# Three changes of order in a hybrid encoder layer: where weight sums are made, when v's tiles are asked for, and where the sums of the branches stand

## The chip, the cores and the metric

The kernel runs on one core of one Trainium2 chip. The metric is the device time of one execution in microseconds. An execution uses five engines: TensorE (PE, matmuls and transposes), VectorE (DVE), ScalarE (ACT), GpSimd (POOL), and SyncE (SP), which here only issues DMAs. Each engine takes its instructions in its own order, and waits at an instruction until what it needs is there.

## The reference

One layer of an encoder, for one sequence of 1024 tokens of width 2048, all in fp32:

```python
h = rmsnorm(x, pre_g) * (1.0 + scale[:, None]) + shift[:, None]   # scale, shift, gate from c
proj = h @ w_in                                                   # 2048 x 4608
q, k, v, gate_a, u, gate_p = jnp.split(proj, SPLIT_POINTS, axis=-1)
y_a = windowed_gqa(q, k, v, rel_table, sink) * jax.nn.silu(gate_a)
y_p = multiscale_pool(u, w_pool_grp, pool_scale) * jax.nn.silu(gate_p)
g = jax.nn.sigmoid(h @ w_merge + b_merge)                         # 2048 x 4096
g_a, g_p = jnp.split(g, N_BRANCHES, axis=-1)
merged = g_a * (y_a @ w_br_attn) + g_p * (y_p @ w_br_pool)        # each 1024 x 2048
o = merged @ w_out                                                # 2048 x 2048
return x + gate[:, None] * rmsnorm(o, post_g)
```

`windowed_gqa` has 8 query heads and 2 key/value heads of 128 and sees 128 tokens to each side; `multiscale_pool` averages over windows of 2, 4, 8 and 16 tokens.

## The kernel before

**Products.** A fp32 operand is split into a high part (`whi`, `T1h`, made by ACT, L95) and a low part (`wlo`, `T1l`, made by DVE, L96), and a product takes three matmuls for each K-tile: high by high, low by high, high by low. Blocks of 2 x 2 are multiplied with seven products instead of eight (`strassen`, L210): B11, T3, T2, B21, T4, T1 and B22, named after the moving operand. Each has four K-tiles of 128 x 512, so 12 matmuls. One call handles one pair of 128-wide columns. Before the products, the weights are combined (`ws`, sums over `raw`, L102 and L105); after them, the results in the banks X, V and Z are read and added into tiles `u`, `p` and `c`, and stored. The matmuls are on L235. The `u<-V,u` of these pages is the sum that reads T4's result from bank V and so frees the bank for the T3 product of the next pair.

**Stages.** Pass 1 (`pass1`, L607) multiplies the first half of the K-tiles of `w_in` and `w_merge` and stores partial sums in `part_d`. In its last pairs, the *x stage*, the second half of x is brought in: `fetch_x` loads a tile `xt` (L762) and scales it on ACT (L763), `turn_x` transposes it on PE (L769) and copies the result out (L772). Tiles `xt` have three buffers, and a tile is loaded two steps ahead of its turn. Pass 2 multiplies the second half of the K-tiles, adds the partial sums and stores `proj_d`; attention and pooling run beside it as further small steps. The attention's k and v are taken by `take_kv`, which loads 128 x 512 tiles `kvr` (L823) and, for v, transposes them (L828). At the end of pass 2 the rows of the attention branch (`ya_d`) are loaded as tiles `y` (L1026) and their operand sums are made (`pre_op`, L147 and L1030). Then come the two branch products, `w_branch_attn` (beside which the pooled branch's tiles, from `yp_d`, are loaded and summed) and `w_branch_pool`, each with gates `gt` (load L1096, sigmoid L1102) that `finish` multiplies with the results (L1112, L1116). The last product, by `w_out`, uses sums of its weights that were made earlier.

**Sums of weights.** `weight_sums` (L629) makes those: `fetch` loads four tiles `sw` of `w_out` (L638), `make` forms four sums on DVE in a pinned order, `put_by` stores them to `ws_d` (L650). `lay_out` says at which product each of the three runs:

```python
for at, step in zip((0, 5, 7), sums.popleft()):
    steps.setdefault(first + (last - first) * k // n + at, []).append(step)
```

With seven products to a pair, `first` 0 and `last` 35 mean that the k-th group of sums is fetched at the first product of pair k, made at its sixth and stored at the first of the next pair.

**Who sets the order.** `run` (L321) calls one product after the other, and behind each the steps that were laid out for it and, for the indices in `every`, one step of a queue `side`. In the x stage `every` is `(0, 1, 2, 4, 5, 6)`: the fourth product has no step of x. The tile framework then schedules each engine's instructions from the traced program. `keep` (L90) pins an instruction: it may not be moved ahead of the instruction of its engine that was traced before it. SP issues all the loads and stores in one queue.

Of the kernel before, what the change touches and what calls it, by code (L numbers as in the profile page):

```python
# [12 lines left out]
F32 = mybir.dt.float32  # L13
F32R = mybir.dt.float32r
AF = mybir.ActivationFunctionType
ALU = mybir.AluOpType
# [4 lines left out]
P = 128  # L21
# [21 lines left out]
def encoder_layer(ctx: ExitStack, tc: tile.TileContext, x, c, table, w_ada, b_ada, pre_g,  # L43
# [32 lines left out]
    def uid(s):  # L76
        cnt[0] += 1
        return f"{s}_{cnt[0]}"
# [11 lines left out]
    def keep(ins):  # L90

        tc.keep_in_program_order(ins)
# [11 lines left out]
    def sub(o, a, b):  # L104
        return nc.vector.tensor_tensor(o, a, b, ALU.subtract)  # L105
# [38 lines left out]
    def new_op(n=4):  # L144
        return {m: [None] * n for m in MOVING}

    def pre_op(j, h1, h2, tmp):  # L147

        sub(h1[j][1], h1[j][1], h1[j][0])
        t2 = tmp()  # L150
        sub(t2, h2[j][1], h1[j][1])
        return t2

    def fill_op(op, js, h1, h2, t2, now=3):
# [452 lines left out]
    def pass1(n, side, every, steps={}):  # L607

        nonlocal i
        for k in range(n):  # L610
            if not ready:
                fetch_pair(i)
            at = [(at, step) for at in range(7) for step in steps.get(7 * k + at, ())]
            if i + 1 < PAIRS:
                at.append((2, lambda i=i: fetch_pair(i + 1)))
            w, n0 = weight_of(ORDER[i])
            run(strassen(w, n0, rows_in_turn(0), range(4), op, ev, to_dram(block(part_d, ORDER[i])),
                         raws=ready.pop(0)), side, every[k % len(every)], at)
            i += 1
        flush()  # L620
# [115 lines left out]
    def lay_out(n, first, last):  # L736

        steps = {}
        for k in range(n):
            for at, step in zip((0, 5, 7), sums.popleft()):  # L740
                steps.setdefault(first + (last - first) * k // n + at, []).append(step)
        assert max(steps) < last + 2
        return steps
# [43 lines left out]
        t2[j] = pre_op(j, h1, h2, lambda: wsp.tile([P, 512], F32, tag="sw", name=uid("tf")))  # L787

    side.extend(lambda j=j: pre(j) for j in range(4))
    pass1(PAIRS - i, side, ((0, 1, 2, 4, 5, 6),), lay_out(5, 0, 35))  # L790
    assert not side and not sums


# [17 lines left out]
    mid.close()  # L811

    with pool("attn") as ap:
        kv = {}

        def take_kv(kvh, what):
            hi = ap.tile([P, S], F32R, tag=what + "hi", name=uid(what))
            lo = ap.tile([P, S], F32R, tag=what + "lo", name=uid(what))
            col = (COL_K if what == "k" else COL_V) + kvh * P
            for s in range(2):  # L820
                sl = slice(s * 512, (s + 1) * 512)
                raw = ap.tile([P, 512], F32, tag="raw", name=uid("kvr"), bufs=2)
                load(raw, proj_d[col:col + P, sl])  # L823
                src = raw
                if what == "v":
                    src = bank("at")
                    for j in range(4):
                        nc.tensor.transpose(src[:, j * P:(j + 1) * P], raw[:, j * P:(j + 1) * P], ident)  # L828
                split(hi[:, sl], lo[:, sl], src)
            kv[what] = (hi, lo)  # L830
# [85 lines left out]
        def step(u, e):  # L916
            nu = len(UNITS)
            if e == 0 and 0 <= u - LAG_V < nu:
                values(u - LAG_V)
            if 0 <= u - LAG_T < nu:  # L920
                turn(u - LAG_T, e)
            if u < nu:
                if u % 16 == 0 and e == 0:
                    take_kv(UNITS[u][0] * 2 // GQA, "k")
                if u % 4 == 0:
                    split_q(e)
                scores(u, e)
            if e == 1:
                if u % 4 == 3 and u + 1 < nu:
                    fetch_q(u + 1)  # L930
                c_ = u - LAG_V + 1
                if 0 <= c_ < nu:
                    if c_ % 16 == 0:
                        take_kv(UNITS[c_][0] * 2 // GQA, "v")
                    if c_ % 4 == 0:
                        open_gate(c_)
# [86 lines left out]
    def y_steps(yd, store_to):  # L1023
        def get(k, s):
            t = sp.tile([P, 512], F32, tag="y", name=uid("y"), bufs=16)
            load(t, yd[k * P:(k + 1) * P, s * 512:(s + 1) * 512])  # L1026
            h1, h2, _ = store_to
            (h1 if k < 4 else h2).setdefault(k % 4, []).append(t)

        def pre(j):  # L1030
            h1, h2, t2 = store_to
            t2[j] = pre_op(j, h1, h2, lambda: sp.tile([P, 512], F32, tag="tf", name=uid("tf"), bufs=4))

        return [lambda k=k, s=s: get(k, s) for k in (0, 4, 1, 5, 2, 6, 3, 7) for s in range(2)] + \
            [lambda j=j: pre(j) for j in range(4)]
# [28 lines left out]
    for b, w in enumerate((w_ba, w_bp)):  # L1064
        op = new_op()
        fill_op(op, range(4), *ys[b], now=7 if b else 3)
        if b == 0:
            side.extend(y_steps(yp_d, ys[1]))
        else:
            ysrc.close()  # L1070
            ev_ctx.close()
            ev_ctx = ExitStack()
            ev = ctx.enter_context(pool("ev4", 4, side="right"))
            mr = ctx.enter_context(pool("mraw", side="right"))

# [12 lines left out]
            mt, mt2 = merged_tiles(), {}  # L1088
            side.extend([lambda: None] * 25)
            for jp in range(JP - 1):  # L1090
                side[6 * jp + 7] = lambda jp=jp: merged_sums(mt, mt2, jp)
        gates, shut = {}, deque()

        def fetch_gate(i, blk, b=b):
            gt = ev.tile([P, 512], F32, tag="gt", name=uid("gt"), bufs=4)
            load(gt, block(proj_d, NIN + b * D + i * 256)(blk))  # L1096
            gates[i, blk] = gt
            shut.append((gt, 64 + b * KT + 2 * i + (1 if blk[0] == "2" else 0)))

        def open_gate():  # L1100
            gt, col = shut.popleft()
            nc.scalar.activation(gt, gt, AF.Sigmoid, bias=cols[:, col:col + 1])  # L1102

        wanted = deque((i, blk) for i in range(8) for blk in ("11", "21", "22", "12"))
        for _ in range(4):
            fetch_gate(*wanted.popleft())

        for i in range(8):
            def finish(blk, ps, addend, res, gates=gates, shut=shut, open_gate=open_gate, i=i, b=b):
                gt = gates.pop((i, blk))  # L1110
                if ps is not None and addend is None:
                    nc.vector.tensor_tensor(res, ps, gt, ALU.mult)  # L1112
                else:
                    if ps is not None:
                        add(res, ps, addend)
                    nc.vector.tensor_tensor(res, res, gt, ALU.mult)  # L1116
                if b == 0:
                    store(block(mp_d, i * 256)(blk), res)
                else:
                    if blk[1] == "1":  # L1120
                        dst = mt[int(blk[0]) - 1][i // 2][:, i % 2]
                    else:
                        dst = ev.tile([P, 512], F32, tag="pv", name=uid("pv"), bufs=2)
                    load(dst, block(mp_d, i * 256)(blk))
                    add(dst, dst, res)
                    if blk[1] == "2":
                        store(block(m_d, i * 256)(blk), dst)
                if shut:
                    open_gate()
                if wanted:  # L1130
                    fetch_gate(*wanted.popleft())

            at = [(n, open_gate) for n in (0, 1, 2, 3)] if i == 0 else []
            if b == 1 and i == 7:
                at += [(1 + jp, lambda jp=jp: put_op(0, jp, ops[0], mt, mt2)) for jp in range(JP - 1)]
                at += [(5, lambda: merged_sums(mt, mt2, JP - 1)), (5, lambda: put_op(0, JP - 1, ops[0], mt, mt2))]
            run(strassen(w, i * 256, rows_apart, range(4), op, ev, finish), side,
                () if b == 0 and i == 0 else (0, 2, 4) if b == 0 or i < 7 else (0, 1, 2, 3), at)
        flush()
        assert not side  # L1140
# [292 lines left out]
```

## Time and profile before

| what | value |
|---|---|
| median of 3 runs | 2140.0 us (2134.43 to 2148.4) |
| the profiled execution | 2138.01 us, span 2136.2 us |
| granted TensorE clock, mean | 0.998 |
| busy, share of the span | PE 98%, DVE 72%, ACT 53% |
| DMA | 466.10 MB, mean 218 GB/s |

Times in the profile count from the start of the span. A row of a timeline reads: start, duration, engine, line, operation, output and inputs, count, and in brackets the idle time of the engine before it with what ended that time. A wait is charged to the last thing that arrived.

### The profile page before, as it was taken

Reading aid. Unit: us, or ns where it says so; the run is one execution under the profiler, and the core shown is the slowest. Engines: PE = TensorE matmul, PEld = TensorE weight load, DVE = VectorE, ACT = ScalarE, POOL = GpSimd, SP = SyncE. Lnnn points to the kernel's source line nnn. Section 1 sums busy time; section 2 is a strip of 40 time slices with the busy share of each in tenths; the row PEclk is TensorE's granted clock in tenths of the full one; section 3 lists DMA queues with packets and bytes.
Section 4 is the critical chain, followed back from the end, with each engine's and each line's share of the span. In section 5 each row is a group of like instructions: output and inputs, shape, how many; then the busy total and the mean of one; then the engine's idle time right before and its main releaser. Section 6 shows DMA issues by size and latency. Waiting matters only on the chain.

```text
span 2136.2 us, 28939 instructions
## 1 busy us (share of the span) xinstructions
PE 2094.8 (98%) x9567; PEld 1715.6 (80%) x9567; DVE 1537.5 (72%) x2754; ACT 1129.4 (53%) x2124; POOL 7.4 (0%) x66
## 2 busy tenths in 40 slices
PE   6999999999999999999999999999999999999998
PEld 3588888888878888888888888878788888788886
DVE  5786666777547677777776888656966977879667
ACT  5654444444474546767775433333645644767655
POOL 0000000000000000000000000000000000000000
PEclk9999999999999999999999999999999999999999
DMA  9886567899676355545445766765654655696997
GB/s 328 269 274 216 187 202 230 300 310 305 214 228 205 119 174 198 169 152 193 157 157 166 231 219 208 229 189 172 222 172 163 220 191 164 212 306 219 301 304 252
DMA packets 303254, 466.10 MB, mean 218 GB/s; under 512 B 23882, under 2 KB 144866, under 8 KB 303104
## 3 DMA queue, kind: packets, MB, share of 16 engines
q1 hardware_dynamic: 301648, 462.02, 66.4%
q0 software_dynamic: 1120, 2.19, 0.3%
q8 instruction: 75, 1.23, 0.2%
q14 instruction: 75, 0.61, 0.1%
q10 hardware_dynamic: 336, 0.06, 0.0%
HBM read 340.41 MB, written 125.85 MB: 218 GB/s over the span
## 4 chain that ended last, share of the span: by engine, by line
PE 89%; DMA 5%; DVE 4%; ACT 1%; issue 1%; SPq 0%; DVEq 0%; ACTq 0%
PE Z L235 30%; PE V L235 20%; PE X L235 20%; PE Z L1163 2%; PE Z L1164 2%; PE Z L1165 2%; PE V L1165 1%; PE V L1163 1%; PE V L1164 1%; PE X L1165 1%; PE X L1164 1%; PE GEMV L453 1%; PE X L1163 1%; DVE wlo L96 1%; DMA xt<-in_x_dram 1%
## 5 line engine op out<-in xcount | busy, mean ns | idle before, releaser
L95 ACT ACTIVATE whi<-raw 128x512 fp32r<-128x512 f32 (+1 forms) x528 | 319.8, 609 | 502.0 <-PE Z L235 254.3
L96 DVE TENSOR_TENSOR wlo<-raw,whi 128x512 fp32r<-128x512 f32 (+1 forms) x528 | 347.6, 663 | 192.6 <-PE Z L235 118.0
L96 DVE TENSOR_TENSOR wlo<-wr,whi 128x512 fp32r<-128x512 f32 x224 | 151.2, 689 | 59.0 <-ACT whi L95 54.9
L95 ACT ACTIVATE whi<-wr 128x512 fp32r<-128x512 f32 x224 | 138.6, 629 | 90.1 <-DVE wlo L96 31.4
L102 DVE TENSOR_TENSOR raw<-raw,raw 128x512 f32<-128x512 f32 x80 | 55.2, 690 | 95.1 <-DMA raw<-in_w_merge_dram 69.3
L1102 ACT ACTIVATE gt<-gt,cols 128x512 f32<-128x512 f32 x64 | 46.1, 722 | 95.3 <-DMA gt<-proj_d 83.3
L235 PE MATMUL V<-T3h,whi 128*128 128x512 f32 x336 | 92.3, 393 | 1.8 <-DVE u L102 1.8
L235 PE MATMUL X<-B11h,whi 128*128 128x512 f32 x336 | 92.5, 393 | 1.1 <-DVE part L102 1.0
L235 PE MATMUL Z<-B22h,whi 128*128 128x512 f32 x336 | 92.4, 395 | 0.6 <-ACT u L290 0.6
L235 PE MATMUL Z<-T1h,whi 128*128 128x512 f32 x336 | 91.5, 391 | 0.6 <-ACT T1h L95 0.6
L235 PE MATMUL Z<-T2h,whi 128*128 128x512 f32 x336 | 92.0, 393 | 0.0
L235 PE MATMUL V<-T4h,whi 128*128 128x512 f32 x336 | 91.5, 391 | 0.4 <-ACT T4h L95 0.4
L102 DVE TENSOR_TENSOR u<-V,u 128x512 f32<-128x512 f32 x94 | 64.7, 688 | 37.7 <-PE V L235 37.0
L235 PE MATMUL V<-T3h,wlo 128*128 128x512 f32 x336 | 91.4, 392 | 0.0
L235 PE MATMUL Z<-T2l,whi 128*128 128x512 f32 x336 | 91.4, 392 | 0.0
L235 PE MATMUL Z<-T1l,whi 128*128 128x512 f32 x336 | 90.9, 390 | 0.3 <-DVE T1l L96 0.3
L235 PE MATMUL V<-T3l,whi 128*128 128x512 f32 x336 | 91.0, 391 | 0.0
L235 PE MATMUL X<-B21h,whi 128*128 128x512 f32 x336 | 91.0, 391 | 0.0
L235 PE MATMUL Z<-T2h,wlo 128*128 128x512 f32 x336 | 90.9, 391 | 0.0
L235 PE MATMUL V<-T4l,whi 128*128 128x512 f32 x336 | 90.9, 390 | 0.0
L235 PE MATMUL X<-B11l,whi 128*128 128x512 f32 x336 | 90.9, 390 | 0.0
L235 PE MATMUL Z<-B22l,whi 128*128 128x512 f32 x336 | 90.7, 390 | 0.0
(306 smaller groups left out, 4872.4 us busy)
## 6 DMA issues: line engine op xcount, KB each, us to landing
part<-part_d SPq DMA_DIRECT2D x136, 256.0 KB, 5.0
ada<-in_w_ada_dram SPq DMA_DIRECT2D x128, 256.0 KB, 5.4
raw<-in_w_in_dram SPq DMA_DIRECT2D x64, 512.0 KB, 4.1
raw<-in_w_merge_dram SPq DMA_DIRECT2D x64, 512.0 KB, 5.6
wr<-ws_dS SPq DMA_DIRECT2D x64, 512.0 KB, 5.2
wr<-in_w_out_dram SPq DMA_DIRECT2D x48, 512.0 KB, 5.1
proj_d<-part SPq DMA_DIRECT2D x68, 256.0 KB, 2.2
sw<-in_w_out_dram SPq DMA_DIRECT2D x64, 256.0 KB, 5.3
```

The lines of the kernel that those rows point to most:

```text
L95: ins = (nc.scalar.activation(hi, src, AF.Copy), nc.vector.tensor_tensor(lo, src, f32(hi), ALU.subtract))
L96: nc.vector.tensor_tensor(lo, src, f32(hi), ALU.subtract))
L102: return (eng or nc.vector).tensor_tensor(o, a, b, ALU.add)
L235: nc.tensor.matmul(ps, w_[:, i], op[mov][j][m_], start=fresh and i == 0 and n == 0, stop=i == nj - 1 and n == 2, skip_group_check=True)
L453: ins = nc.tensor.matmul(pv[g:g + 32, :], scz[:, kc, :], tile_of(kc), start=kc < 4, stop=kc >= 12, tile_position=(0, g))
L1102: nc.scalar.activation(gt, gt, AF.Sigmoid, bias=cols[:, col:col + 1])
L1163: nc.tensor.matmul(pb, hi, w[0], start=first, stop=False, skip_group_check=True)
L1164: nc.tensor.matmul(pb, lo, w[0], start=False, stop=False, skip_group_check=True)
L1165: nc.tensor.matmul(pb, hi, w[1], start=False, stop=last, skip_group_check=True)
```

## The change

There are three edits. First, the weight sums of the x stage move by three products: `lay_out(5, 0, 35)` becomes `lay_out(5, 3, 38)`, so that a group is fetched at the fourth product of a pair, made at the second product of the next and stored at its fourth. Second, the raw tiles of v are loaded by a new `fetch_v`, called one step before `take_kv` uses them. Third, the sums of `y` and the multiplies by the gates are pinned with `keep`: `pre_op` gets a parameter `pin`, which the x stage leaves empty.

```diff
-    def pre_op(j, h1, h2, tmp):
-
-        sub(h1[j][1], h1[j][1], h1[j][0])
+    def pre_op(j, h1, h2, tmp, pin=lambda ins: None):
+
+        pin(sub(h1[j][1], h1[j][1], h1[j][0]))
         t2 = tmp()
-        sub(t2, h2[j][1], h1[j][1])
+        pin(sub(t2, h2[j][1], h1[j][1]))
         return t2
...
-    pass1(PAIRS - i, side, ((0, 1, 2, 4, 5, 6),), lay_out(5, 0, 35))
+    pass1(PAIRS - i, side, ((0, 1, 2, 4, 5, 6),), lay_out(5, 3, 38))
...
-        kv = {}
+        kv, vraw = {}, []
+
+        def fetch_v(kvh):
+            for s in range(2):
+                vraw.append(ap.tile([P, 512], F32, tag="raw", name=uid("kvr"), bufs=2))
+                load(vraw[s], proj_d[COL_V + kvh * P:COL_V + (kvh + 1) * P, s * 512:(s + 1) * 512])
...
-                raw = ap.tile([P, 512], F32, tag="raw", name=uid("kvr"), bufs=2)
-                load(raw, proj_d[col:col + P, sl])
-                src = raw
-                if what == "v":
-                    src = bank("at")
+                if what == "k":
+                    src = raw = ap.tile([P, 512], F32, tag="raw", name=uid("kvr"), bufs=2)
+                    load(raw, proj_d[COL_K + kvh * P:COL_K + (kvh + 1) * P, sl])
+                else:
+                    raw, src = vraw.pop(0), bank("at")
...
                 c_ = u - LAG_V + 1
+                if (c_ + 1) % 16 == 0 and c_ + 1 < nu:
+                    fetch_v(UNITS[c_ + 1][0] * 2 // GQA)
...
-            t2[j] = pre_op(j, h1, h2, lambda: sp.tile([P, 512], F32, tag="tf", name=uid("tf"), bufs=4))
+            t2[j] = pre_op(j, h1, h2, lambda: sp.tile([P, 512], F32, tag="tf", name=uid("tf"), bufs=4), keep)
...
-                    nc.vector.tensor_tensor(res, ps, gt, ALU.mult)
+                    keep(nc.vector.tensor_tensor(res, ps, gt, ALU.mult))
...
-                    nc.vector.tensor_tensor(res, res, gt, ALU.mult)
+                    keep(nc.vector.tensor_tensor(res, res, gt, ALU.mult))
```

No instruction is added or removed on PE, DVE, ACT or SP; their order changes in three places. In the attention stage no row changes its place.

**Place one: SP in the x stage**, around the loads of the sixth and seventh x tile. Before, where these are called `xt_5500` and `xt_5544` (`sw` are weights and their sums, `raw` weights of the pass, `ws_dS_95` to `ws_dS_98` the four sums in memory):

```order
L762 DMA xt_5500<-in_x_dram 128x512
L311 DMA part_d<-u_1128_5411 128x512
L650 DMA ws_dS_97<-sw_5345 128x512
L650 DMA ws_dS_96<-sw_5463 128x512
L650 DMA ws_dS_95<-sw_5343 128x512
L650 DMA ws_dS_98<-sw_5349 128x512
L311 DMA part_d<-p_1120_5372 128x512
L638 DMA sw_5536<-in_w_out_dram 128x512
L638 DMA sw_5538<-in_w_out_dram 128x512
L638 DMA sw_5540<-in_w_out_dram 128x512
L638 DMA sw_5542<-in_w_out_dram 128x512
L762 DMA xt_5544<-in_x_dram 128x512
```

With the change, where the same two tiles are called `xt_5495` and `xt_5527`:

```order
L650 DMA ws_dS_97<-sw_5407 128x512
L650 DMA ws_dS_96<-sw_5559 128x512
L650 DMA ws_dS_95<-sw_5405 128x512
L311 DMA part_d<-u_1124_5403 128x512
L762 DMA xt_5495<-in_x_dram 128x512
L187 DMA raw_5597<-in_w_merge_dram 128x4x256
L762 DMA xt_5527<-in_x_dram 128x512
L311 DMA part_d<-p_1116_5364 128x512
L650 DMA ws_dS_98<-sw_5411 128x512
L638 DMA sw_5635<-in_w_out_dram 128x512
L762 DMA xt_5564<-in_x_dram 128x512
L638 DMA sw_5637<-in_w_out_dram 128x512
```

The second tile's load stood behind four stores of sums and four loads of weights, and now stands ahead of the store of `p`, the fourth store and all the loads; the first tile's load now stands behind three stores and the store of `u`. On DVE three or four of a group's four sums, which all stood behind `u<-V,u`, now stand ahead of it: they are pinned behind the low part of the weights of the next pair's T3 product (`wlo<-ws`), which is prepared that early.

**Place two: DVE at the end of pass 2**, around `u<-V,u` of the pair in which the attention branch's sums are traced. Before:

```order
L105 TENSOR_TENSOR y_13066<-y_13066,y_13044 128x512
L102 TENSOR_TENSOR u_2593_12948<-V_12856,u_2593_12948 128x512
L96 TENSOR_TENSOR wlo_13069<-raw_12844,whi_13068 128x512
L105 TENSOR_TENSOR tf_13411<-y_13109,y_13066 128x512
L96 TENSOR_TENSOR wlo_13091<-raw_13012,whi_13090 128x512
L102 TENSOR_TENSOR p_2586_12892<-p_2586_12892,u_2600_13004 128x512
L105 TENSOR_TENSOR y_13150<-y_13150,y_13130 128x512
L96 TENSOR_TENSOR wlo_13112<-raw_13014,whi_13111 128x512
```

With the change:

```order
L105 TENSOR_TENSOR ws_13208<-raw_13174 128x512
L102 TENSOR_TENSOR u_2593_12948<-V_12856,u_2593_12948 128x512
L96 TENSOR_TENSOR wlo_13069<-raw_12844,whi_13068 128x512
L96 TENSOR_TENSOR wlo_13091<-raw_13012,whi_13090 128x512
L102 TENSOR_TENSOR p_2586_12892<-p_2586_12892,u_2600_13004 128x512
L96 TENSOR_TENSOR wlo_13112<-raw_13014,whi_13111 128x512
```

All eight sums (four `y<-y,y`, four `tf<-y,y`) have left this pair and the next; they stand some 30 to 50 rows further down, in the pair after.

**Place three: the pooled branch's sums.** On DVE in the first pair of `w_branch_attn`, before:

```order
L105 TENSOR_TENSOR tf_15253<-y_14564,y_14447 128x512
L96 TENSOR_TENSOR T4l_14249<-y_13271,T4h_14248 128x512
L1112 TENSOR_TENSOR c_14311<-X_14179,gt_14167 128x512
L96 TENSOR_TENSOR T4l_14253<-y_13368,T4h_14252 128x512
L105 TENSOR_TENSOR y_14653<-y_14653,y_14608 128x512
L96 TENSOR_TENSOR T1l_14279<-y_13066,T1h_14278 128x512
L102 TENSOR_TENSOR u_2869_14276<-V_14181,u_2869_14276 128x512
```

With the change:

```order
L96 TENSOR_TENSOR T4l_14249<-y_13271,T4h_14248 128x512
L1118 TENSOR_TENSOR c_14311<-X_14179,gt_14167 128x512
L96 TENSOR_TENSOR T4l_14253<-y_13368,T4h_14252 128x512
L96 TENSOR_TENSOR T1l_14279<-y_13066,T1h_14278 128x512
L96 TENSOR_TENSOR wlo_14387<-raw_14379,whi_14386 128x512
L96 TENSOR_TENSOR T1l_14283<-y_13150,T1h_14282 128x512
L102 TENSOR_TENSOR u_2869_14276<-V_14181,u_2869_14276 128x512
```

The sums `y` and `tf` of this pair and the following ones, eight in all, now stand later: six in the last pair of `w_branch_attn`, and two, `y_15091` and `tf_15417`, among the low parts of the first pair of `w_branch_pool`. On PE the T1 product of that pair, before, ran through in one piece (four `T1h`, four `T1l`, four `T1h`). With the change it reads:

```order
L235 MATMUL Z_15668<-T1h_15611,whi_15777 128x512
L235 MATMUL X_15808<-B11h_15519,whi_15811 128x512
L235 MATMUL X_15808<-B11h_15524,whi_15811 128x512
L235 MATMUL Z_15668<-T1h_15615,whi_15777 128x512
L235 MATMUL X_15808<-B11h_15529,whi_15811 128x512
L235 MATMUL X_15808<-B11h_15534,whi_15811 128x512
L235 MATMUL X_15808<-B11l_15520,whi_15811 128x512
L235 MATMUL X_15808<-B11l_15525,whi_15811 128x512
L235 MATMUL X_15808<-B11l_15530,whi_15811 128x512
L235 MATMUL X_15808<-B11l_15535,whi_15811 128x512
L235 MATMUL Z_15668<-T1h_15619,whi_15777 128x512
L235 MATMUL Z_15668<-T1l_15608,whi_15777 128x512
```

Eight matmuls of the next pair's B11 product have moved in between T1's, ahead of its last `T1h` and of all the `T1l`.

More of the change, by code (lines that the diff above doesn't have):

```diff
@@ L818, in take_kv @@
             lo = ap.tile([P, S], F32R, tag=what + "lo", name=uid(what))
-            col = (COL_K if what == "k" else COL_V) + kvh * P
             for s in range(2):
                 sl = slice(s * 512, (s + 1) * 512)
-                raw = ap.tile([P, 512], F32, tag="raw", name=uid("kvr"), bufs=2)
-                load(raw, proj_d[col:col + P, sl])
-                src = raw
-                if what == "v":
-                    src = bank("at")
+                if what == "k":
[3 more added lines that the diff above has]
+                    raw, src = vraw.pop(0), bank("at")
                     for j in range(4):
```

## Prediction

> **What bounds the kernel now.** I read the page first: busy time and the chain that ended last.
>
> ```profile
> span 2136.2 us, 28939 instructions
> PE 2094.8 (98%) x9567; PEld 1715.6 (80%) x9567; DVE 1537.5 (72%) x2754; ACT 1129.4 (53%) x2124; POOL 7.4 (0%) x66
> PE 89%; DMA 5%; DVE 4%; ACT 1%; issue 1%; SPq 0%; DVEq 0%; ACTq 0%
> ```
>
> TensorE is busy for 98% of the span and makes up 89% of the chain. The diff neither removes nor adds a matmul. So the change can only give back idle time of TensorE, or make new idle time. The waits of that engine say how much there is.
>
> ```profile
> PE XT L405 <- DVE turn L397: 11.4, 4, 9.1
> PE b L769 <- ACT xt L763: 4.1, 2, 2.3
> PE V L235 <- DVE u L102: 1.8, 1, 1.8
> PE b L828 <- DVE pp L96: 1.2, 1, 1.2
> PE Z L235 <- ACT T1h L95: 0.6, 1, 0.6
> PE V L235 <- ACT T4h L95: 0.4, 1, 0.4
> PE Z L235 <- DVE T1l L96: 0.3, 1, 0.3
> ```
>
> The columns after the colon are total, times and longest. The first row is the start of the program, which the diff does not touch. The other six are the places that its edits border on, and they sum to 8.4 us. The clock comes on top of it.
>
> ```profile
> 610.00:614.00 4.00, 4.00 (x14) 3.18 (x13) 1.38 (x2) 3.32 (x10) 0.00 (x0) 0.57 0.63 171
> 634.00:638.00 4.00, 2.38 (x13) 2.05 (x14) 1.26 (x2) 3.00 (x8) 0.00 (x0) 1.00 0.77 259
> 1394.00:1399.00 5.00, 4.96 (x15) 3.98 (x16) 2.37 (x4) 0.63 (x1) 0.00 (x0) 0.66 0.75 158
> ```
>
> In these windows the third number from the end is TensorE's granted clock. After the first late x tile it is 0.57 over 4 us, which loses (1 - 0.57) x 4 = 1.72 us of matmul time. After the wait for `u` it is 0.66 over 5 us, a loss of 1.70 us. After the second late x tile it stays at 1.00. So the idle time and the slow clock behind it are worth some 12 us in all, 0.6% of the run: that is the ceiling.
>
> **Edit 1, the weight sums of the x stage.** These are the two late x tiles:
>
> ```profile
> 606.77 1.07 PE L235 MATMUL Z<-B22h,wlo 128*128 128x512 f32 x4
> 609.71 0.66 PE L769 MATMUL b<-ident,xt 128*128 128x128 f32 x4 [1.88 <-ACT xt L763]
> ...
> 631.38 1.08 PE L235 MATMUL Z<-B22l,whi 128*128 128x512 f32 x4
> 632.29 1.07 PE L235 MATMUL Z<-B22h,wlo 128*128 128x512 f32 x4
> 635.62 0.55 PE L769 MATMUL b<-ident,xt 128*128 128x128 f32 x3 [2.26 <-ACT xt L763]
> ```
>
> Ends of matmuls are modelled, so I count from starts. Four undisturbed matmuls take 0.91 us (631.38 to 632.29). The transposes were due at 607.68 and came at 609.71: 2.03 us late. The second group was due at 633.20 and came at 635.62: 2.42 us late. Why the tile was late stands in SP's queue and at ACT.
>
> ```profile
> 598.12 0.60 PE L769 MATMUL b<-ident,xt 128*128 128x128 f32 x4
> 595.56 0.33 SPq L762 DMA_DIRECT2D xt<-in_x_dram  x1
> 596.46 2.84 SPq L650 DMA_DIRECT2D ws_dS<-sw  x4
> 601.08 0.32 SPq L311 DMA_DIRECT2D part_d<-p  x1
> 601.46 1.88 SPq L638 DMA_DIRECT2D sw<-in_w_out_dram  x4
> 603.38 0.90 SPq L762 DMA_DIRECT2D xt<-in_x_dram  x2
> 608.94 0.72 ACT L763 ACTIVATE xt<-xt,rstd 128x512 f32<-128x512 f32 x1 [2.98 <-DMA xt<-in_x_dram]
> ```
>
> The tile's buffer came free with the transposes at 598.12, about 598.5. Its load was issued only at 603.38. Four stores of weight sums, which wait for VectorE's sums, the store of `p` and four weight loads stood ahead of it. In the new order this load stands behind three sum stores, the store of `u`, one x load and one weight load, and ahead of `p`, the fourth sum store and the loads of weights. All four sums of this group now stand ahead of `u<-V,u` on VectorE, 4 x 0.6 us against its idle 1.70 us (595.13 below). So the first three stores go at about 594 to 596, that of `u` at about 596.5, and the x load can follow its buffer at 598.5. With the landing time of x tiles (row below) it arrives near 603.8, at the worst 605.3, and is scaled 0.72 us later: 1.6 to 3.1 us ahead of the 607.68 at which it is wanted. The same holds one pair on. Gain 2.03 + 1.72 + 2.42 = **6.2 us**. At worst nothing is gained.
>
> ```profile
> DMA to landing us min/median/max: 3.1/5.3/6.8
> 595.13 0.69 DVE L102 TENSOR_TENSOR u<-V,u 128x512 f32<-128x512 f32 x1 [1.70 <-PE V L235]
> 601.66 0.70 PE L235 MATMUL V<-T3h,whi 128*128 128x512 f32 x2
> ```
>
> What it costs: the sums take 0.7 us more than the idle time, so `u` comes at most about 0.7 us later. Its bank is wanted again at 601.66, 5.8 us after `u` ended, so this is hidden. The x tile before, issued at 595.56, now goes after `u`, about 1.4 us later; it is turned behind the T3 product that starts at 601.66 and takes 3 x 0.91 us, so near 604.4. Issued near 597, it lands by 602.3 at the median and is scaled by 603.0: 1.4 us early. Nothing is paid there.
>
> **Edit 2, v's raw tiles a step ahead.** Nothing moves: in the attention stage no row of SP, TensorE, VectorE or ACT changes its place, because the loads wait for the same buffers that q and k use. The nearest wait is `PE b L828 <- DVE pp`, which is for a bank and not for the load. I count 0; if a load did become late, the nearest bound is that wait's own size, 1.2 us either way.
>
> **Edit 3, sums pinned in traced place.** At the end of the second pass the attention branch's sums (`y`, `tf`) stood on VectorE ahead of work that TensorE needs.
>
> ```profile
> 1369.73 0.69 DVE L105 TENSOR_TENSOR y<-y,y 128x512 f32<-128x512 f32 x1 [3.05 <-DMA y<-ya_d]
> 1370.34 0.69 DVE L102 TENSOR_TENSOR u<-V,u 128x512 f32<-128x512 f32 x1
> ...
> 1392.60 0.69 DVE L105 TENSOR_TENSOR ws<-raw 128x512 f32<-128x512 f32 x1 [1.13 <-DMA raw<-in_w_merge_dram]
> 1393.21 0.69 DVE L102 TENSOR_TENSOR u<-V,u 128x512 f32<-128x512 f32 x1
> ...
> 1391.13 1.07 PE L235 MATMUL X<-B11h,wlo 128*128 128x512 f32 x4
> 1394.04 1.15 PE L235 MATMUL V<-T3h,whi 128*128 128x512 f32 x4 [1.85 <-DVE u L102]
> ```
>
> A sum waits 3.05 us for its `y`, `u` runs behind it, the stores and weight loads behind `u` on SP go late, and 20 us on a weight load lands so late that `ws` and then `u` hold up T3: due at 1392.04, begun at 1394.04, 2.00 us late, with 1.70 us of slow clock behind it. In the new order all eight sums stand one pair later, and `u` follows V directly. The chain then starts up to 3.05 us earlier; at least the two sums ahead of the p store, 2 x 0.6 = 1.2 us, are out of it. The stall vanishes from 2.00 us on. That lies between the bounds, and I take, near the middle, the chain as some 2.3 us earlier, which clears it with 0.3 us to spare. Because that is thin I count **3.0** of the 3.7 us; the bounds are 0 and 3.7.
>
> The pooled branch's sums leave the first pair of the next stage, where one waited for its data and held the T1 tiles. That is the three small waits of the list above, 0.6 + 0.4 + 0.3 = **1.3 us**, and no clock was lost there. Here ACT's tiles also come ahead of a gate that waits for its DMA; the bounds are 0 and 1.3.
>
> ```profile
> 1525.38 0.69 DVE L105 TENSOR_TENSOR y<-y,y 128x512 f32<-128x512 f32 x1 [1.89 <-DMA y<-yp_d]
> 1527.59 0.72 ACT L1102 ACTIVATE gt<-gt,cols 128x512 f32<-128x512 f32 x1 [1.52 <-DMA gt<-proj_d]
> ...
> 1645.00:1688.00 43.00, 43.00 (x190) 35.09 (x189) 42.75 (x71) 32.58 (x59) 0.00 (x0) 1.00 0.50 163
> 1679.83 0.68 DVE L96 TENSOR_TENSOR T1l<-y,T1h 128x512 fp32r<-128x512 f32 x1
> 1679.92 1.14 PE L235 MATMUL Z<-T1l,whi 128*128 128x512 f32 x4
> ```
>
> Six of them go to where VectorE has gaps. Two go into 1645 to 1688, where it is busy for 42.75 of 43 us at 0.60 us an instruction. With one more row that also moves ahead, the last T1l ends 3 x 0.6 = 1.8 us later, near 1682.3. Today it is used at about 1680.6, which would be a stall. But TensorE's new order puts eight `X<-B11` matmuls (1.8 us) in front of it, so it is wanted near 1682.4. I count 0; without that cover it is 1.7 us, and as much again if the clock drops. The pinned gate multiplies keep their neighbours: 0.
>
> **Sum.** 6.2 + 3.0 + 1.3 = 10.5 us. The profiled run took 2138.0 us for its span of 2136.2; 2138.0 - 10.5 = 2127.5 us. The median of the three runs is 2140.0, 2 us above the profiled one, and they spread from 2134.4 to 2148.4, so I put the forecast at **2127.5** and the run's own noise into the range.
>
> [...] The row first: half clock followed 1.88 and 1.85 us of idle time, and did not follow 2.26 us. [...]
>
> **The rivals.**
> 1. *The wait for `u` stays on the weight load.* `ws<-raw` still stands ahead of `u` and waited 1.13 us for the load. If the load is less than 2.00 us earlier, part of the stall and its clock loss remain: 2138.0 - 6.2 - 1.3 = 2130.5. For it: the load's landing decides, and my margin is 0.3 us.
> 2. *The x tiles stay late*, the edit does not do what it says: the load moves up in the queue but waits for another one ahead of it. Then 2138.0 - 4.3 = 2133.7. Against it: 1.6 to 3.1 us of margin.
> 3. *The slow clock is not the stalls' doing.* If the drop has another cause it stays where it was, or comes back after another gap: the sum keeps 2.03 + 2.42 + 2.00 + 1.3 = 7.8 us and gives 2130.2. For it: 2.26 us of idle time cost no clock. Against it: both drops stand in the window right behind such a gap.
> 4. *T1 of the pooled branch stalls*, with the clock: +1.7 + 1.7, giving 2130.9.
> 5. *Slower: the sums block `u`.* The weight sums now stand ahead of `u<-V,u` in each pair of the x stage, and VectorE takes its work in order. If the weights land late, `u`, its store and bank V wait with them, and TensorE stalls at T3. It decides where a sum's weights land more than 5 us behind their place (5.8 us of slack less the sum). The two late groups start 25.91 us apart, of which 4.1 were lost, so a pair takes 21.8 us; the sums after 592.7 come again near 614.5. Weights issued near 603 would have to take some 16 us. Each of the four pairs then pays the excess, 2 us say, and 1.7 us of clock: 4 x 3.7 = 14.8 us, and 2138.0 - 10.5 + 14.8 = 2142.3. Against it: 4.1 us is the usual way of such transfers.
>
> ```profile
> DMA to landing us min/median/max: 2.1/4.1/6.2
> ```
>
> That row is for the tiles `sw` between 560 and 700 us.
>
> **How the numbers follow.** Forecast 0.5; rivals 1 to 5: 0.19, 0.1, 0.09, 0.07, 0.05. The cases lie between 2126.8 (all of the 3.7 us) and 2142.3; with the spread of runs, -5.6 and +8.4 around their median, 8 in 10 lie between 2118 and 2140. A measurement of this kernel can tell about 1% from no change, 21 us. The ceiling of 12 us is below that, so "within 1%" holds nearly all: 0.91. Faster by more than 1% (below 2118.6) needs a fast draw on top of the full gain: 0.06. Slower by more than 1% (above 2161) needs the fifth rival at more than twice its price: 0.03.
>
> **What would show it.** Edit 1 is right if no wait `PE b L769 <- ACT xt` is left and the clock near 610 is 1.00. Edit 3 is right if `PE V L235 <- DVE u` is gone near 1390 and the three small waits near 1525 are. Edit 2 is right if the wait at L828 stays about 1.2 us. I am wrong if one of these waits stands elsewhere: at T3 in the x stage (rival 5), at T1 near 1680 (rival 4), or if the clock halves at a place with no wait.

## The result and the profile after

The changed kernel takes 2132.4 us at the median of 12 runs (2130.06 to 2135.59), against 2141.03 us for the kernel before (2134.43 to 2148.4, 12 runs): a ratio of 0.996, with a 95% interval of 0.995 to 0.9971. It is 8.6 us faster, where 2127.5 us and a gain of 10.5 us on the profiled run were forecast. A second series gave 2129.36 against 2138.8 us, ratio 0.9957 (0.9941 to 0.9972). The profiled execution took 2130.95 us, 7.1 us less than that of before.

The page's first line and waits of TensorE (total, times, longest in us; the start of the program and the last product are left out). The count of instructions is two below that of before (28939), and the difference is in semaphore instructions alone:

```profile
span 2129.2 us, 28937 instructions
...
PE X L235 <- DVE part L102: 2.1, 1, 2.1
PE b L832 <- DVE pp L96: 1.4, 1, 1.4
...
PE PV L911 <- DVE pp L96: 1.2, 3, 0.6
...
PE PV L910 <- ACT pp L95: 0.9, 1, 0.9
PE Z L235 <- ACT whi L95: 0.8, 1, 0.8
PE V L235 <- DVE u L102: 0.6, 2, 0.3
```

The wait of the transposes on `xt` (4.1 us) is gone, that of T3 on `u` is down from 1.8 us to two waits of 0.3 us, and the three small waits on T1 and T4 tiles are gone. Others have grown or come: `X` on `part` from 1.0 to 2.1 us, `PV` on `pp` from 0.5 to 2.1 us in two rows, and a new `Z` on `whi` of 0.8 us.

In the x stage, SP's queue, ACT and TensorE now read:

```profile
593.23 2.25 SPq L650 DMA_DIRECT2D ws_dS<-sw  x3
...
596.78 0.39 SPq L762 DMA_DIRECT2D xt<-in_x_dram  x1
...
598.64 0.38 SPq L762 DMA_DIRECT2D xt<-in_x_dram  x1
...
605.30 0.73 ACT L763 ACTIVATE xt<-xt,rstd 128x512 f32<-128x512 f32 x1 [2.34 <-DMA xt<-in_x_dram]
...
607.58 0.60 PE L769 MATMUL b<-ident,xt 128*128 128x128 f32 x4
...
610.00:614.00 4.00, 4.00 (x22) 3.32 (x21) 1.35 (x3) 3.78 (x11) 0.00 (x0) 1.00 0.74 222
```

The tile's load is issued at 598.64, against 603.38 before. It is scaled at 605.30 and transposed at 607.58 with no wait, 1.6 us after its scaling ended. The clock stays at 1.00 where it was 0.57.

At the end of pass 2, the weight load on SP before and after, and then VectorE and TensorE after:

```profile
1386.20 0.38 SPq L187 DMA_DIRECT2D raw<-in_w_merge_dram  x1
...
1380.60 0.38 SPq L187 DMA_DIRECT2D raw<-in_w_merge_dram  x1
...
1387.60 0.69 DVE L105 TENSOR_TENSOR ws<-raw 128x512 f32<-128x512 f32 x1 [5.29 <-DMA raw<-in_w_merge_dram]
1388.21 0.68 DVE L102 TENSOR_TENSOR u<-V,u 128x512 f32<-128x512 f32 x1
...
1387.67 1.07 PE L235 MATMUL X<-B11h,wlo 128*128 128x512 f32 x4
1389.04 1.17 PE L235 MATMUL V<-T3h,whi 128*128 128x512 f32 x4 [0.30 <-DVE u L102]
```

T3 was due at 1388.58 and began at 1389.04, 0.46 us late instead of 2.00. The same wait for a weight load still stands ahead of `u`, and still ends a little too late. The load is now issued 8.0 us ahead of T3's due time (1380.60), before 5.8 us (1386.20 against 1392.04).

Setting the same matmul of both traces side by side, by starts, shows where the time went between the two profiled runs:

| place (us, after) | forecast | shift, us |
|---|---|---|
| late x tiles, 607 and 629 | -4.45 | -2.13, -2.45 |
| slow clock behind the first | -1.72 | -1.6 |
| T3 on `u`, 1389, and the clock behind | -3.0 | -1.6, -1.6 |
| three waits, 1515 to 1522 | -1.3 | -2.0 |
| `PV` on `pp`, 932 | 0 | +1.5 |
| `X` on `part`, 1323 | 0 | +1.1 |
| `Z` on `whi` for T2, 1683 | 0 | +1.2 |
| `Z` on B22's low part, 1528 | 0 | +0.6 |
| all, with what is smaller and the start | -10.5 | -7.0 |

So the parts that were forecast gave 11.4 us in this pair of traces, and some 4.4 us stand against them. The experiments ask which of these belong to the change.

### The profile page after: what moved, and what is told of

It reads as the page before. It is cut to its first block, busy times and chain, and to the rows that moved or that the text cites. A ratio compares the mean times of both kernels' runs of the same rounds, so it can differ in the third digit from the quotient of the medians.

```text
span 2129.2 us, 28937 instructions
## 1 busy us (share of the span) xinstructions
PE 2090.4 (98%) x9567; PEld 1714.1 (81%) x9567; DVE 1536.9 (72%) x2754; ACT 1129.4 (53%) x2124; POOL 7.4 (0%) x66
## 3 DMA queue, kind: packets, MB, share of 16 engines
q0 software_dynamic: 1120, 2.19, 0.3%
## 4 chain that ended last, share of the span: by engine, by line
PE 84%; DMA 6%; DVE 6%; ACT 2%; issue 1%; SPq 0%; ACTq 0%; DVEq 0%; POOLq 0%
PE Z L235 28%; PE V L235 19%; PE X L235 18%; PE Z L1169 2%; PE Z L1170 2%; PE Z L1171 2%; PE V L1169 1%; PE V L1171 1%; PE V L1170 1%; DVE wlo L96 1%; PE X L1171 1%; PE X L1170 1%; PE X L1169 1%; PE GEMV L453 1%; DMA raw<-in_w_merge_dram 1%
## 5 line engine op out<-in xcount | busy, mean ns | idle before, releaser
L235 PE MATMUL X<-B11h,wlo 128*128 128x512 f32 x336 | 90.9, 390 | 0.0
L235 PE MATMUL X<-B21l,whi 128*128 128x512 f32 x336 | 90.8, 389 | 0.0
L235 PE MATMUL Z<-T1h,wlo 128*128 128x512 f32 x336 | 90.6, 389 | 0.0
```

The lines of the kernel that those rows point to most:

```text
L235: nc.tensor.matmul(ps, w_[:, i], op[mov][j][m_], start=fresh and i == 0 and n == 0, stop=i == nj - 1 and n == 2, skip_group_check=True)
```

## The experiments

**The parts.** The kernel before with the call to `fetch_v` and the split of `take_kv` alone is built into the same rows with the same waits as before on all five engines, and so is the kernel with the pins on the gate multiplies alone. They are the same program, so they were not run. What is left of the change is the move of the weight sums and the pins on the sums of `y`.

*The weight sums alone.*

```diff
-    pass1(PAIRS - i, side, ((0, 1, 2, 4, 5, 6),), lay_out(5, 0, 35))
+    pass1(PAIRS - i, side, ((0, 1, 2, 4, 5, 6),), lay_out(5, 3, 38))
```

> The kernel before with the weight sums moved by three products, and nothing else. Theory: the two late x tiles are gone (no wait of the transposes at L769 on ACT's xt; before 1.9 and 2.3 us), with the slow clock behind the first; the T3 product near 1388 still waits about 2 us for u; all else stays. Time 4.5 to 6.2 us below before (4.5 without a clock loss), ratio 0.997 to 0.998. Rival, the gain is given back: since TensorE runs about 6 us ahead of the DMAs' timing, the waits near 932 (PV on pp) and 1323 (X on DVE's part) are larger than before, by 1.9 and 1.3 us as in the changed kernel, and the time is only 1 to 3 us below before.

Measured: 2132.29 against 2138.8 us, ratio 0.9974 (0.9964 to 0.9983), so 5.6 us. Its waits of TensorE have no row of L769:

```profile
PE X L235 <- DVE part L102: 0.9, 1, 0.9
PE V L235 <- ACT Z L273: 0.7, 1, 0.7
```

The late tiles are gone. T3 near 1388 lost only 0.9 us by the starts, and to a copy on ACT, where about 2 us for `u` were expected, though no sum of `y` is pinned here: the wait on `u` varies from run to run. `X` on `part` has its old size, so this does not grow because TensorE runs ahead. `PV` on `pp` is 1.1 us, against 0.5 before and 2.1 in the changed kernel.

*The pins alone* (`pre_op` with `pin`, `keep` from `y_steps`, as in the change).

> The kernel before with the sums of y pinned in both branches, and nothing else. Theory: the wait of T3 on u near 1394 falls from 1.9 us to at most 0.4 us with its slow clock, the three small waits near 1525 (0.6, 0.4, 0.3 us) go, a wait of Z<-T2h near 1690 of about 0.8 us comes; the late x tiles stay at 1.9 and 2.3 us. Time 3 to 5 us below before, ratio 0.9975 to 0.9985. The waits near 937 and 1326: if they grow because TensorE runs ahead after the x stage, they are here as before (none and 1.0 us); if they vary by chance, they may be larger here too.

Measured: 2136.75 against 2138.8 us, ratio 0.9989 (0.9977 to 1.0001): 2.4 us, not quite clear of zero, and under the expected 3 to 5.

```profile
PE b L769 <- ACT xt L763: 4.1, 2, 2.8
PE PV L907 <- DVE pp L96: 1.0, 2, 0.6
PE PV L906 <- ACT pp L95: 0.8, 2, 0.6
PE V L235 <- DVE u L102: 0.8, 1, 0.8
PE Z L235 <- ACT whi L95: 0.7, 1, 0.7
```

The three small waits are gone, the T2 wait on `whi` has come with these pins, and the late tiles stay. The wait on `u` is 0.8 us, more than the 0.4 expected. `PV` on `pp` is there, 1.8 us in two rows, with TensorE not ahead at all, and up to the end of the attention stage this kernel's rows are those of the kernel before. So it is not given-back time of the x stage. The two parts add up within their intervals: 5.6 + 2.4 = 8.0 us, against 8.6 and 9.2 for the whole.

*The changed kernel again.*

> The changed kernel once more. If the waits near 932 (PV on pp, 0.9 and 0.6 us) and 1323 (X on DVE's part, 2.1 us) come with the new order, they stand here again with these sizes; if they are chance of the transfers' timing, they are gone or elsewhere. The wait of Z<-T2h near 1683 (0.8 us) comes from the new order of VectorE and ACT and must stand here again. Time as the changed kernel's, 2132 us, 8 to 9 us below before.

Measured: 2129.36 us, ratio 0.9957 (0.9941 to 0.9972).

```profile
PE PV L911 <- DVE pp L96: 0.9, 2, 0.5
PE X L235 <- DVE part L102: 0.9, 1, 0.9
PE Z L235 <- ACT whi L95: 0.8, 1, 0.8
...
PE PV L910 <- ACT pp L95: 0.5, 1, 0.5
```

`X` on `part` is 0.9 us, so the 2.1 was chance. `PV` on `pp` stands again, with 1.4 us instead of 2.1. The T2 wait stands again with the same size: it belongs to the order.

*The kernel before, twice more.*

> The kernel before once more, for a second profile of its waits. [...] Rival, the first profile is typical: u's wait is 1.8 to 2.0 us with a drop behind it, and pinning the attention branch's sums is worth 3.7 us. The wait of PV on pp near 937 shows whether it belongs to the program before too: about 1.5 us if so, none if the change made it.

> [...]

Measured: 2139.2 and 2134.5 us. First the one, then the other:

```profile
PE b L769 <- ACT xt L763: 3.5, 2, 2.2
PE V L235 <- DVE u L102: 2.6, 2, 1.4
...
PE Z L235 <- ACT T1h L95: 0.9, 1, 0.9
PE PV L907 <- DVE pp L96: 0.7, 2, 0.6
```

```profile
PE b L769 <- ACT xt L763: 4.1, 2, 2.3
PE V L235 <- DVE u L102: 1.9, 1, 1.9
PE Z L235 <- ACT T1h L95: 1.6, 1, 1.6
```

The late tiles are a fixture of the program, 3.5 to 4.1 us in four profiles with the old order of sums. Near 1390, T3 was late by 2.0, 1.3 and 2.05 us by the starts in three runs of the kernel before (of the 2.6 us in the second, 1.4 are at 500 us). The wait on T1 was 0.6, 0.9 and 1.6 us. `PV` on `pp` belongs to the program too, with 0.7 and 0.6 us. With the 1.8 us of the pins alone, whose rows are the same up to there, its size in the order of before is anything from 0.5 to 1.8 us. That the changed kernel has 2.1 and 1.4 us is therefore not shown to be the change's doing, though these few profiles can't exclude a part. Behind these gaps the granted clock was 0.57 over 610 to 614 us and 0.66 over 1394 to 1399 us in the first profile, 0.50 over 635.78 to 639.20 us in the second (behind the other x tile), and 1.00 over 1389.30 to 1392.70 us, behind T3's gap, in the third.

**The pooled branch's pins.**

*Without them.* `y_steps` gets the pin as a parameter, and the pooled branch passes none:

```diff
-            side.extend(y_steps(yp_d, ys[1]))
+            side.extend(y_steps(yp_d, ys[1], lambda ins: None))
```

> The changed kernel with the pins on the attention branch's sums only; the pooled branch's sums stand where they stood before. Theory: the wait of Z<-T2h on ACT's whi near 1683 (0.8 us) goes, since VectorE's full stretch has no added sums, and the three waits near 1522 to 1530 (together 1.9 us by the starts) are back: 1 us above the changed kernel, 2130 to 2133 us, ratio about 0.9965. Rival: that wait stays, then it comes from something else, and the time is 2 us above the changed kernel.

Measured: 2132.68 us, ratio 0.9975 (0.9963 to 0.9986) to its before of 2137.69.

```profile
PE V L235 <- DVE u L102: 1.9, 2, 1.1
PE Z L235 <- ACT T1h L95: 1.5, 1, 1.5
...
PE V L235 <- ACT T4h L95: 0.4, 1, 0.4
```

The T2 wait on `whi` is gone, and the waits on T1 and T4 are back with 1.9 us. What the pooled pins gain there is partly paid back by the T2 wait. The time alone can't part this kernel from the changed one.

*All eight sums one pair earlier.*

```diff
-                () if b == 0 and i == 0 else (0, 2, 4) if b == 0 or i < 7 else (0, 1, 2, 3), at)
+                () if b == 0 and i == 0 else (0, 2, 4, 6) if b == 0 else (0, 2, 4) if i < 7 else (0, 1, 2, 3), at)
```

> The changed kernel, but the steps of the pooled branch's rows run on four products of each pair instead of three, so that all eight sums stand in the sixth pair of w_branch_attn and none in the full stretch of VectorE. Theory: the wait of Z<-T2h near 1683 (0.8 us) goes and the first pair of w_branch_attn stays without waits: 0.5 to 1.3 us below the changed kernel. Rival: the full stretch of VectorE is not what makes that wait (ACT's weights are late there for another reason), and it stays at 0.8 us with the time unchanged.

Measured: 2131.24 us, ratio 0.9963 (0.9948 to 0.9977). The wait of Z on `whi` is gone, as expected, and the first pair of `w_branch_attn` has no wait. The 0.5 to 1.3 us of gain can't be seen in the time: its interval and that of the changed kernel in the same series overlap. Why VectorE's full stretch makes ACT late, by the rows of the kernel before (the first two) and of the changed kernel:

```profile
1684.79 0.32 SPq L1096 DMA_DIRECT2D gt<-proj_d  x1
1688.13 0.72 ACT L1102 ACTIVATE gt<-gt,cols 128x512 f32<-128x512 f32 x1 [2.76 <-DMA gt<-proj_d]
...
1677.91 0.68 DVE L1122 TENSOR_TENSOR p<-p,gt 128x512 f32<-128x512 f32 x1
1678.62 0.32 SPq L1102 DMA_DIRECT2D gt<-proj_d  x1
1680.92 0.69 DVE L105 TENSOR_TENSOR raw<-raw 128x512 f32<-128x512 f32 x1
1681.67 0.72 ACT L1108 ACTIVATE gt<-gt,cols 128x512 f32<-128x512 f32 x1 [1.56 <-DVE raw L105]
1682.30 2.18 ACT L95 ACTIVATE whi<-raw 128x512 fp32r<-128x512 f32 x4
...
1682.96 1.20 PE L235 MATMUL Z<-T2h,whi 128*128 128x512 f32 x4 [0.77 <-ACT whi L95]
```

ACT's row `gt<-gt,cols` stands ahead of its split of the weights, and T2 waits for the split. T2 was due at 1682.03 (0.91 us after the last row of B22 began, at 1681.12), and in the kernel before at 1690.04, where it was on time. By the trace the gate's load waits on SP for the multiply `p<-p,gt`, which frees its buffer. With the fuller stretch the load goes out 3.4 us ahead of T2's due time and no longer 5.2 us, so the row starts 0.4 us ahead of it and no longer 1.9, and the split after it is late. The trace charges ACT's wait to VectorE's weight sum `raw`, which is late behind the stretch too, but the row does not read it. The gate's load landed within 0.1 us of that sum's end, and in the run with two products below, which has the same order there, the same wait (1.39 us) is charged to the load. Both come late through VectorE's stretch; which of the two ended last is not settled.

**Is it the place in the queue?**

*The x tiles on GpSimd's queue*, in the kernel before:

```diff
-        load(xt, x[si * P:(si + 1) * P, c0:c0 + 512])
+        nc.gpsimd.dma_start(xt, x[si * P:(si + 1) * P, c0:c0 + 512])
```

> The kernel before, with the x tiles of the x stage loaded through GpSimd's queue and not SP's; weight sums where they were. Theory: it is the place in SP's queue that makes two x tiles late, so both waits at L769 (1.9 and 2.3 us) go although the sums' stores and the weight loads stay where they are; the T3 wait near 1390 and the waits near 1525 stay. Rival, the transfers are the limit in that stretch (the DMA engines were busy for 0.8 to 1.0 of 596 to 610 us): the tiles still land late, by 1 us or more.

Measured: 2157.48 us in one run. This did not answer the question. The scheduler moved the x steps with the load: all sixteen tiles, transposed from 585.8 us on before, come bunched between 638.9 and 672.1 us.

*The weight sums on GpSimd's queue*, loads and stores of the last five groups, in the kernel before:

```diff
+        late_group = i * (KT // 2) + j >= 11
+        q = nc.gpsimd.dma_start if late_group else load
...
-                load(a[name], wo_rows(kh)[:, j, n0:n0 + 512])
+                q(a[name], wo_rows(kh)[:, j, n0:n0 + 512])
...
-                store(ws_rows(name)[:, j, i * 512:(i + 1) * 512], t)
+                q(ws_rows(name)[:, j, i * 512:(i + 1) * 512], t)
```

> The kernel before, with the last five groups of weight sums loaded and stored through GpSimd's queue; they are made where they were and move the same bytes, and SP's queue then has no weight of theirs ahead of an x tile. Theory, place in the queue: the seventh x tile is loaded when its buffer comes free (about 598.5), both waits at L769 (together 4 us) are gone, and the time is that of the weight sums' move alone, ratio 0.997 to 0.998. Rival, the transfers: the same loads compete for the DMA engines and the tile still lands late, with a wait of over 1 us at L769 left. The wait on u near 1390 and the three near 1525 stay either way.

Measured: 2139.39 against 2137.86 us, ratio 1.0009 (0.9994 to 1.0024). SP's queue, the tile's scaling, its transposes, and then the place where the gain went:

```profile
599.74 0.33 SPq L764 DMA_DIRECT2D xt<-in_x_dram  x1
...
606.58 0.72 ACT L765 ACTIVATE xt<-xt,rstd 128x512 f32<-128x512 f32 x1 [4.31 <-DMA xt<-in_x_dram]
...
608.68 0.60 PE L771 MATMUL b<-ident,xt 128*128 128x128 f32 x4
...
667.59 0.69 DVE L105 TENSOR_TENSOR ws<-raw 128x512 f32<-128x512 f32 x1 [5.63 <-DMA raw<-in_w_merge_dram]
...
668.94 1.20 PE L235 MATMUL V<-T3h,whi 128*128 128x512 f32 x4 [3.75 <-DVE u L102]
```

Both late tiles are gone: the load goes as soon as its buffer is free (it now stands ahead of the store of `p` too), and the transposes wait for nothing. The transfer itself was no faster: from its load to its scaling the tile took 5.6 us before (603.38 to 608.94), 6.7 us in the changed kernel and 6.8 us here. Only the load is earlier, so the cause is the place in SP's queue. One thing differs besides: on GpSimd three of the four weight loads went out later, at 603.98 to 607.17, behind the landing of the stores. The time did not follow (its forecast, a ratio of 0.997 to 0.998, was missed), because a new wait of 3.75 us came further on, with slower matmuls behind it (a `T3l` matmul at 669.98 took 0.59 us, where one at 654.83 took 0.39): a weight load landed late, and `ws` held up `u`. It is the mechanism of 1394 us in the kernel before, in another place. What made this load late was not tried.

*Two products instead of three.* The edit is `lay_out(5, 2, 37)`.

> The changed kernel with the weight sums moved by two products instead of three (the sums are made at the first product of a pair). The load of the seventh x tile then stands behind four sum stores, u's store and two weight loads, but the sums are made 3 us earlier on VectorE. Theory: what counts is when the queue is free for that load, about 599 us, so it lands by 605 and no wait at L769 of over 0.4 us comes: same time as the changed kernel, 2130 to 2133 us. Rival, weights ahead of x in the queue are harmful by themselves: a wait of 1 to 2 us at L769 is back.

Measured: 2128.68 us, ratio 0.9956 (0.9941 to 0.9971), as the changed kernel. At L769 one wait of 0.2 us is left, for a copy on ACT and not for a tile. So neither the exact place nor two loads of weights ahead of the tile matter, as long as the queue is free near 599 us.

**The clock.** A probe copies X to Z several times on ACT, so that TensorE waits for the bank:

```diff
-        nc.scalar.activation(bz, bx, AF.Copy)
+        for _ in range(1 + SEEDS.get(pairs_[0], 0)):
+            nc.scalar.activation(bz, bx, AF.Copy)
```

with `SEEDS = {n: 5 + n % 5 for n in range(8, 26)}`.

> The changed kernel, in which 18 pairs of pass 1 copy X to Z not once but 6 to 10 times on ACT, so that TensorE waits there for the bank, some 1 to 4 us at each. [...] Rival, by length alone: every gap above 1.85 us drops the clock. [...]

Only five of the 18 places waited (2139.87 us), 2.9 us in all and 2.1 us at the longest; most of the copies were hidden. The second probe has `8 + n % 6`:

> The clock probe with longer waits: 18 pairs of pass 1 copy X to Z 9 to 14 times. [...] Rival, by length: gaps above 1.9 us all drop the clock. [...]

Measured: 2163.01 us, with a mean granted clock of 0.994. Two stretches with a gap, each with the one behind it (PE busy is the second number, the granted clock the third from the end):

```profile
209.34:212.75 3.41, 0.92 (x4) 0.67 (x4) 1.38 (x2) 2.51 (x5) 0.00 (x0) 1.00 0.68 209
212.75:216.16 3.41, 3.41 (x9) 2.64 (x9) 0.00 (x0) 0.63 (x1) 0.00 (x0) 0.50 0.02 5
417.55:420.97 3.42, 1.74 (x8) 1.12 (x6) 0.85 (x2) 3.29 (x7) 0.00 (x0) 1.00 0.94 317
420.97:424.40 3.43, 2.92 (x13) 2.44 (x14) 0.25 (x1) 1.08 (x2) 0.00 (x0) 1.00 0.93 327
```

TensorE was idle for 73% of the first, and behind it the granted clock was 0.50 over 3.41 us. It was idle for 49% of the third, and behind it the clock was 0.93 over 3.43 us. Then the kernel with the pins alone around its longest gap, of 2.82 us:

```profile
629.16:632.58 3.42, 2.13 (x10) 1.42 (x8) 0.00 (x0) 0.26 (x2) 0.00 (x0) 1.00 0.86 246
632.58:635.99 3.41, 1.88 (x11) 1.63 (x11) 0.75 (x2) 2.65 (x7) 0.00 (x0) 1.00 0.85 280
635.99:639.40 3.41, 3.41 (x17) 2.82 (x16) 2.02 (x3) 2.07 (x6) 0.00 (x0) 1.00 0.76 210
```

TensorE was idle for 38% and 45% of the first two stretches, and the clock stayed at 1.00 in all three. In the second probe matmuls were also slowed behind a wait of only 0.82 us: four at 465.72 took 1.91 us, where four at 460.95 took 1.07. Sixteen one-column matmuls (L703, 1.84 us) stood ahead of that wait. So the rivals by length fall: 1.85 and 1.88 us of idle time were followed by half clock in the kernel before, and 2.82 us were not here. What decides it was not shown.

## Why the prediction was right, and where not

**Edit 1 was right in mechanism and size.** Forecast 6.2 us; the traces show 2.13 + 2.45 + 1.6 = 6.2, and the part by itself measures 5.6 us (3.6 to 7.7 from its interval). The cause, the place in SP's queue, is shown by the sums taken off it, so the second rival is out. The margin was 1.6 us, at the lower end of the forecast 1.6 to 3.1. The average is a little below 6.2 because the clock does not always drop: it cost 1.7 us in the first profile (0.57 over 610 to 614 us) and in the second (0.50 over 635.78 to 639.20 us), and nothing behind the 2.82 us of the pins alone (1.00).

**Edit 2 was right**: nothing moved. The wait at what is now L832 is 1.4 us, as 1.2 before; in the second profiles of both kernels it is 0.4 and 0.2 us, so its size says little.

**Edit 3, `u` at the end of pass 2: the mechanism was right, the term was too large.** 3.0 us were counted from one profile, with a wait of 2.00 us and 1.70 us of clock. Over the six profiles without these pins T3 was late by 0.9 to 2.05 us, 1.6 on average by the starts, and by my count the clock halved behind two of them (it was 0.66 over 1394 to 1399 us in the first profile, and 1.00 over 1389.30 to 1392.70 us in the third). Over the eight with them it was late by 0 to 1.25 us, 0.5 on average, and in the five that I followed to 1412 us no matmul behind it was slowed (a group of four every 0.90 to 1.01 us). From these rows and that count I estimate 1.1 + 1.7 x 2/6 = 1.7 us. The step that failed is the use of one profile's wait and clock loss as if they were typical. A second slip is in "some 2.3 us earlier, which clears it": the weight load was indeed issued earlier against T3's due time, 7.9 us ahead of it over the eight profiles and 6.0 us over the six, but from its issue to `ws` it then took 6.9 us instead of 6.2. Of the 1.9 us, 1.2 were left. So the margin of 0.3 us came out as 0.46 us late, and the first rival holds in part: the wait on the weight load stayed.

**Edit 3, the pooled sums: gain undersized, cost missed.** The three waits gave 2.0 us, where the list of waits had shown 1.3. The 1.8 us by which two sums and one more row lengthen VectorE's full stretch did not stall T1, as forecast. They stalled the next thing, the weights of T2: by 0.6 to 0.9 us at its first matmul in the six profiles with this order, and by 1.2 us in all in the first pair of traces. The step that failed is the "I count 0" for these two sums: it looked for T1's cover and not for what is late next behind it. The fourth rival had asked for a stall near this place, but of T1, at 1.7 us and as much again for the clock; product and price were others, and no clock was lost. That the term still came out near its 1.3 us (2.0 less 1.2) is luck: two errors that cancel.

**The time.** 2132.4 us is 4.9 us above the forecast 2127.5. Only 1.9 us of this are the gain. The other 3.0 us are the base: the 10.5 us were taken off the profiled execution of 2138.0 us, and the median of 12 runs before is 2141.0. The prediction also took 1% as the least that a measurement can tell from no change. With 12 runs of each kernel the interval is 0.995 to 0.9971, so 0.4% stands clear.

**The third rival** asked whether the clock's loss belongs to the gaps. In the traces half clock came behind gaps, but not behind each: it followed 1.88 and 1.85 us in the kernel before and 2.19 us in its second profile (0.50 over 635.78 to 639.20 us), and not 2.26 us in the kernel before or 2.82 us with the pins alone (1.00 behind both). What else decides was not shown. Nor is the loss shown to be gone for good with these gaps: in the profiled run with two products, where TensorE waited 1.7 us in the last product, which no edit touches, the mean granted clock was 0.997, against 0.998 in the first profiles of both kernels.

**The slower rival** did not happen in the changed kernel. The run with the sums off SP showed its kin at 3.75 us, `u` late behind work ahead of it on VectorE, though behind `ws` and not behind a weight sum.

The sum of the parts as measured, 5.6 for the x stage and 2.4 for the pins, is 8.0 us against the 8.6 us of the whole. `PV` on `pp` and `X` on `part`, which took 2.6 us from the first pair of traces, stand in the order of before as well, with sizes that vary from profile to profile.

## What to carry to other kernels

Order a shared DMA queue by when each item can start and when it is wanted: a store that waits for an engine should not stand ahead of a load whose buffer is already free (here such a load went out at 603.38 instead of 598.64 us, and TensorE waited 2.03 us). A wait read from a single profile has a size by chance as well as a cause (T3's was 0.9 to 2.05 us in six profiles); before counting it in full, look at it in a second profile, and count a lost clock by its odds. When work is moved into a stretch where an engine has no gaps, look past the nearest consumer to the next one that waits for the engine's later results (here the weights of T2, late by 0.6 to 0.9 us).

## What the runs showed of the hardware

The granted clock was 0.50 over 3.41 us from 610.45 and from 1395.51 us in the kernel before, and over 635.78 to 639.20 us in its second profile, each time behind a gap of 1.85 to 2.19 us; 3.41 us at 0.50 are 1.7 us of matmul time. It stayed at 1.00 behind gaps of 2.26 us in the kernel before, 1.89 us in its third profile and 2.82 us with the pins alone. So a gap of about 2 us cost nothing or 1.7 us, and what decides it was not shown. Three such gaps at 1.7 us each are some 5 us that may or may not be lost. This estimate can account for a part of the kernel's wider range of times before (14.0 us, against 5.5 us for the changed kernel, in 12 runs each); that it does was not shown.
